# Telling TensorE's sequencer ahead of time which way each expert pair's branch goes

## The chip, the cores and the metric

The kernel runs on one core of one Trainium2 chip. The metric is the device time of one execution in microseconds (us), median of the runs shown. TensorE, VectorE, ScalarE, GpSimd and SyncE (the queue that issues most transfers) each have a sequencer of their own, which reads that engine's instruction stream, takes its branches, and hands the work to the engine.

## The reference, cut to what matters

One layer of a hybrid backbone over 256 latent tokens of 1024 channels. A first half (convolution branch, neighbourhood attention branch, recurrent branch, gates, output projection) is followed by a mixture of experts, which is where the change lies:

```python
gate = jnp.einsum("blk,blke->ble", w_sel, jax.nn.one_hot(e_idx, N_EXPERTS, dtype=f32)).astype(h.dtype)
out = jnp.zeros_like(h)
for e in range(N_EXPERTS):                       # 16 experts, hidden width 512
    he = jax.nn.silu(h @ w1[e]) * (h @ w3[e])
    out = out + gate[..., e:e + 1] * (he @ w2[e])
```

Each token goes to 2 of the 16 experts (the best two of its best group of four), so an expert gets few of the 256 tokens.

## The kernel before

**Two experts at a time.** The 16 experts are worked off as 8 pairs, p = 0 to 7. Each expert has 64 slots; `gather` fills them with its tokens' channels by products with one-hot matrices. For each pair TensorE makes the first product (`product(p, 0, ph0)`, the slots times w1), the second one (`product(p, 1, ph)`, times w3), turns the hidden rows (`hidden`), multiplies them by w2 (`rows`), and adds the result to the tokens (`scatter`, L1197). Of a product there are 8 steps, one for each 128 channels; in the trace a step is 4 weight loads and 4 matmuls, so a product is 32 of each, all on line L1162. The last pair is done by halves of the columns.

**The pairs overlap.** In the loop over p the first product of pair p + 1 is a generator, `w1`: two of its steps are issued behind `rows(p)`, then comes `scatter(p)`, then the six others, and then the next pass of the loop begins with the branch on pair p + 1.

**The branch.** An expert may get over 64 tokens. `cnt` holds the larger count of each pair. `values_load` puts it into a register of every engine (a TENSOR_LOAD, L1317 or L1322), and `tc.If(counts[p] > 64)` (L1323 for pairs 2 to 6, L1311 through `more` for pairs 0, 1 and 7) chooses. When it holds, `extra(p, 64)` works 32 more slots, and inside it `further(p, 96)`, `further(p, 128)` and so on stand nested, down to 224; each is a branch of its own. When it doesn't hold, every engine has to jump over the code of all six chunks. In `second` the second product stands in both arms of the If; for pairs 0, 1 and 7 the second product stands behind it. With this input one pair (5) has more than 64 tokens and none more than 96.

**The weights.** The experts' weights (192 quarters of a matrix, 512 KB each) go into 35 places, in the order of use. `load_experts` issues as many as `freed(n)` has granted; each issue waits on SyncE's queue until the place's last reader is done, and for an earlier transfer, as eight are under way at most.

Of the kernel before, what the change touches and what calls it, by code (L numbers as in the profile page):

```python
# [18 lines left out]
T = 256  # L19
# [7 lines left out]
# Columns of the packed per-channel vectors.  # L27
# [9 lines left out]
# Column blocks of the input projection, in units of 128.  # L37
CA, CGA, CQ, CK, CV, CRX, CRG, CG = 0, 4, 8, 12, 16, 20, 24, 28

# Places of 4 KB a partition, and of 1 KB and 2 KB for what is short-lived.  # L40
NPC, NRAW, NW, NSG, NSQ = 35, 4, 2, 6, 2
# How far the gates run ahead of their branches, and the scores of the values.
# [8 lines left out]
def tile_kernel(ctx, tc, x_all, cc, vecs, mod_a, mod_b, w_k, w_rx, w_v, w_in, rnn_w, rpb_t, w_br, w_out,  # L51
# [42 lines left out]
    def by4(dt=F32, name="b4"):  # L94
        """Eight blocks of T in two pieces: block k of them is f(k)."""
        ts = [cut(piece(dt, name), 0, [4, T]) for _ in range(2)]
        return lambda k: ts[k // 4][:, k % 4, :]

    # The experts' weights, a quarter of a matrix at a time: [pair][matrix][quarter][expert of the pair].
    ew = [[[[None, None] for _ in range(4)] for _ in range(3)] for _ in range(8)]  # L100
    # Those of the last pair are cut by their columns: half of the first two's come first, a quarter of the third's.
# [3 lines left out]
    # These come last before the experts' turn, into places that are free only then, and for a short while.  # L105
# [11 lines left out]
    def load_experts(n=192):  # L117
        """The next quarters, n at most, as long as there is room."""
        while n and room[0] > 0 and ew_order:
            p, i, q, s = ew_order.pop(0)  # L120
            n_ = loaded[0]
            loaded[0] += 1
            # the places of the other weights take their share
            make = piece if n_ % SPAN < OWN else w_tile if n_ % SPAN < OWN + XW else raw_tile
            load_expert(p, i, q, s, make(F32, "ew"), pool if n_ < OWN else nc.sync)
            room[0] -= 1
            n -= 1

    # The weights in the order in which they are used.
# [14 lines left out]
    # Each gate's projection runs LAG pairs of channel blocks ahead of its branch's product.  # L144
# [15 lines left out]
    # The last modulation weights have places of their own, from when the branches are done with theirs.  # L160
# [10 lines left out]
    # What has been loaded and not been used: weights, and modulation weights.  # L171
# [23 lines left out]
    def split_parts():  # L195
        """The split of the next weights, in two steps."""
# [26 lines left out]
    def load_ma_half(i, j):  # L223
        """Those of one k tile: 128 columns of the scale, and of the shift."""
# [45 lines left out]
    # before[i, j] = j < i, for ties that go to the first  # L270
# [12 lines left out]
    def rsqrt(srcs, n, scale):  # L283
        """1 / sqrt(ps * scale + eps) for n values a partition: a first guess from the bits, then Newton."""
# [13 lines left out]
        # y (15 - 10 x y^2 + 3 x^2 y^4) / 8, left at 8 / 3 of its size  # L298
# [9 lines left out]
    def spread(rs, n, name):  # L308
        """[token, n tiles] as rows of tokens, the same on every partition: [128, n * 128] in PSUM."""
# [20 lines left out]
    # adds the two halves of the rows below, and turns them  # L330
# [4 lines left out]
    class Mod:  # L335
        """Scale and shift of 256 channels, or of half j of them."""
# [6 lines left out]
        def products(self, ns=range(KD // 2)):  # L343
            # even and odd k tiles on different groups of the array's columns
# [54 lines left out]
    class Channels:  # L399
        """The normed tokens' channels of k tile k, in two parts."""  # L400
# [20 lines left out]
    def proj_block(ps, w, k, cols, both, start, stop):  # L421
        """Adds block `cols` of one k tile of the weights to ps: latents, then the context."""
# [6 lines left out]
    # Work of the other engines that fills the time of the projections, in two chains; what has been  # L429
    # asked of TensorE and of VectorE, in us, says when more of it is due.  # L430
# [48 lines left out]
    # The engines' turns, by the order in which the modulation's weights arrive.  # L479
# [46 lines left out]
    def mod_round_b(out, bank):  # L526
        """The modulation of 256 columns of each of the four quarters."""
# [18 lines left out]
    def set_g1(m, col):  # L546
        # half: the gated branches are summed at twice their size
        dve.tensor_scalar(g1[:, m:m + 1], col, v("mod_b", 16 + m), 0.5, op0=ALU.add, op1=ALU.mult)
# [29 lines left out]
    def gated_inputs():  # L578
        """The inputs of the convolution's and of the recurrence's output products."""
# [4 lines left out]
    def taps(b):  # L584
# [3 lines left out]
        for j in range(31):  # L588
            o = j - 15
            if o:  # L590
                # the tokens that have this neighbour
# [76 lines left out]
    def rnn(h):  # L668
        """Both directions of channel blocks 2 h and 2 h + 1."""
# [29 lines left out]
        # together, as they bring in a table of their own  # L699
# [57 lines left out]
    att_out = []  # L757

    def attention():
# [5 lines left out]
        # The heads' sums of squares, each block's on a group of the array's columns: [head, token], then turned.  # L765
# [131 lines left out]
    def shift_sums():  # L897
        """The part of the second norm's shift in the router's sums, the same for every token."""
# [49 lines left out]
    # The second norm's factor is left until the tokens are on partitions, its shift until the channels are.  # L948
# [22 lines left out]
    for m in range(KD):  # L971
# [16 lines left out]
        else:  # L988
            act.activation(sq2, xl[:, m, :], AF.Square)
            # brings in the table that the router's scores need  # L990
# [18 lines left out]
    # The last modulation vector is needed by the experts' rows only.  # L1009
# [21 lines left out]
    def ranks(x, n, name):  # L1031
        """How many of the four come before each one in x [128, n, 4], the first of equals first."""
# [14 lines left out]
    # A group's score is its largest sum of two.  # L1047
# [29 lines left out]
    # The scores and the masks go first.  # L1077
# [21 lines left out]
    def one_hot(e0):  # L1099
        """Slots 1 to 64 of four experts."""  # L1100
# [6 lines left out]
    def gather(oh, w, place):  # L1107
        """The tokens in their w slots: place(k) becomes [channel, w]."""
# [15 lines left out]
    def quarter(p, i, s, k, h):  # L1124
        """Rows k and half h of the columns of a matrix of an expert: its tile, and where in it."""
# [5 lines left out]
    # Room for the experts' rows, and for what leads to them.  # L1131
# [5 lines left out]
    def slots(p, oh, w):  # L1137
        """The slots' tokens, and the weights of the first 2 w slots: w of either expert."""
# [14 lines left out]
    def product(p, i, ph, h=None):  # L1153
        """The slots times one of the two matrices of the hidden rows, or half h of its columns."""
# [18 lines left out]
    def hidden(q):  # L1173
        """Half of the hidden rows, turned."""
# [5 lines left out]
    def rows(p, py, f, q):  # L1180
        """The experts' rows."""
# [8 lines left out]
    def scatter(rows_, toks, ms=range(KD), parts=2):  # L1190
        """The rows, added to the tokens that they belong to."""
# [12 lines left out]
    def extra(p, n, rest_=iter(())):  # L1204
        """Slots n + 1 to n + 32 of experts 2p and 2p + 1. The array's four column groups take an expert and half
        of the columns each. The steps of rest_ fill TensorE's time."""
# [8 lines left out]
        # the slots on partitions, then the channels  # L1215
# [58 lines left out]
        else:  # L1274
            # the places of the rows' parts still hold weights
# [18 lines left out]
    # Pieces that the experts' weights leave to the rest: the tokens, two groups' slots, the rows, the chunks  # L1294
    # beyond the first.
# [11 lines left out]

    def further(p, n):
        """The chunks from slot n + 1 on, as long as there are tokens for them."""
        if n < T:  # L1310
            with tc.If(counts[p] > n):  # L1311
# [3 lines left out]
    def more(p):  # L1315
        """The tokens of pair p beyond the first 64 of an expert."""
        counts[p] = nc.values_load(cnt[0:1, p:p + 1], min_val=0, max_val=T)  # L1317
        further(p, 64)

    def second(p, ph0, ph):  # L1320
        """The second product, and what there is of more(p)."""
        counts[p] = nc.values_load(cnt[0:1, p:p + 1], min_val=0, max_val=T)  # L1322
        with tc.If(counts[p] > 64) as c:  # L1323
# [22 lines left out]
    # The first products follow the tokens' channels.  # L1346
    ph0 = mm_bank(name="ph0")
    opening = open_group(0)
    next(opening)
    w1 = product(0, 0, ph0)  # L1350
# [8 lines left out]
    for p in range(7):  # L1359
# [4 lines left out]
        else:  # L1364
            # before the second product, as places are wanted
# [22 lines left out]
        # the rows' parts are waited for behind a little of the next product  # L1388
        ahead(w1, 2)
        scatter(lambda i, m: ys[i][:, m * 128:m * 128 + 128], lambda m: oT_)  # L1390
        run(w1)

# [34 lines left out]
def layout(x, c, ctx, c_ctx, router_w, router_bias, mod_w, mod_b, norm1_g, norm2_g, in_w, in_b, conv_dw_w,  # L1427
           conv_dw_b, conv_ln_g, conv_ln_b, conv_pw_w, na_q_g, na_k_g, na_rpb, na_out_w, rnn_conv_w,
           rnn_conv_b, rnn_wa, rnn_ba, rnn_wx, rnn_bx, rnn_lam, rnn_out_w, out_w, exp_w1, exp_w3, exp_w2):
    """The inputs as the program reads them; elements are only moved."""  # L1430
# [114 lines left out]
```

## Time and profile before

| | us |
|---|---|
| median of 3 runs | 641.96 |
| lowest and highest run | 639.98, 643.71 |
| span of the profiled execution, from first to last instruction | 640.2 |
| median less that span | 1.8 |
| TensorE busy in it | 586.9 (92%) |
| VectorE, ScalarE, GpSimd busy | 349.3, 260.0, 19.4 |

The trace tells the profiled execution's span; what a run's time has around the span is not in the trace, so the median less the span stands for it. A line of a timeline reads: start, duration, engine, line of the kernel, operation, out<-in by the program's names, partitions x elements, count, and in brackets the time for which the engine was idle before it and what ended that. An engine name with a q (PEq, PEldq, SPq, ACTq) is that engine's sequencer: it loads registers, waits, branches or issues, and the engine does nothing by it. PEld is TensorE loading weights, which overlaps with matmuls.

### The profile page before, as it was taken

What the parts mean: (1) busy time and instruction counts of PE and PEld (TensorE: products, weight loads), DVE (VectorE), ACT (ScalarE), POOL (GpSimd) and SP (SyncE); (2) the same over time, 40 slices, a digit from 0 to 9 for tenths busy, and PEclk for the clock granted to TensorE, in tenths of its full rate; (3) what the DMA queues carried; (4) which work ended last, traced back from release to release, by engine and by line L of the source; (5) the groups of instructions that cost most, each with busy time, mean ns of one, the idle gap of its engine ahead of it and who ended that gap; (6) DMA issues with size and microseconds to landing.
All of it is one profiled execution on the core that took longest, in us unless ns stands there. A gap on an engine that the chain in (4) does not pass through costs nothing. (4 is left out here: it accounts for less than half of the span.)

```text
span 640.2 us, 10603 instructions
## 1 busy us (share of the span) xinstructions
PE 586.9 (92%) x4127; PEld 411.5 (64%) x4127; DVE 349.3 (55%) x797; ACT 260.0 (41%) x456; POOL 19.4 (3%) x42
## 2 busy tenths in 40 slices
PE   1899999999999999999999989898989599998977
PEld 1689888768788869887999843353335245443454
DVE  4667999999688959885686541202221214222303
ACT  4335357373799647876455342021103011030101
POOL 0000000000000001022020100000000000000000
PEclk9999999999999999999999989999999899999979
DMA  8973974336742634679698759999999979489921
GB/s 255 376 305 141 312 249 153 130 138 232 262 162 102 225 138 149 224 283 349 226 346 303 234 216 368 346 334 407 354 407 409 407 252 412 170 298 408 408 109 67
DMA packets 51826, 170.68 MB, mean 267 GB/s; under 512 B 5664, under 2 KB 10016, under 8 KB 51744
## 3 DMA queue, kind: packets, MB, share of 16 engines
q1 hardware_dynamic: 46704, 151.26, 64.1%
q0 software_dynamic: 5040, 18.35, 8.1%
q8 instruction: 48, 0.79, 0.5%
q14 instruction: 34, 0.28, 0.1%
HBM read 168.54 MB, written 1.05 MB: 265 GB/s over the span
## 5 line engine op out<-in xcount | busy, mean ns | idle before, releaser
L1162 PE MATMUL ph<-ew,xg 128*64 128x512 f32 (+1 forms) x576 | 121.6, 570 | 21.3 <-issue 12.2
L1162 PEld LDWEIGHTS ph<-ew,xg 128*64 128x64 f32 x576 | 44.4, 143 | 86.8 <-issue 75.5
L73 ACT ACTIVATE w<-raw 128x1024 fp32r<-128x1024 f32 x68 | 71.8, 1057 | 65.0 <-PE gps L69 11.6
L74 DVE TENSOR_TENSOR w<-raw,w 128x1024 fp32r<-128x1024 f32 x68 | 82.9, 1219 | 21.1 <-ACT w L73 20.5
L1171 DVE SCALAR_TENSOR_TENSOR he<-sl,gsl,ph 128x256 f32<-128x256 f32 x16 | 7.1, 477 | 100.9 <-PE ph L1162 99.9
L70 PE MATMUL gps<-h,w 128*128 128x256 f32 x192 | 55.2, 288 | 1.1 <-DVE w L74 1.1
L68 PE MATMUL gps<-h,w 128*128 128x256 f32 x192 | 55.9, 291 | 0.4 <-DVE y L934 0.4
L69 PE MATMUL gps<-h,w 128*128 128x256 f32 x192 | 54.5, 284 | 0.0
L593 DVE SCALAR_TENSOR_TENSOR cacc<-up,vc,cacc 128x243 f32<-128x243 f32 (+14 forms) x120 | 52.1, 470 | 1.4 <-ACT cacc L585 0.7
L1183 PE MATMUL py<-ew,heT 128*64 128x512 f32 x224 | 49.6, 595 | 1.1 <-ACT heT L1178 0.8
L74 DVE TENSOR_TENSOR ys<-py,ys 128x512 fp32r<-128x512 f32 (+1 forms) x18 | 11.4, 632 | 58.0 <-ACT ys L73 58.0
L68 PEld LDWEIGHTS gps<-h,w 128*128 128x128 f32 x192 | 36.6, 191 | 4.1 <-issue 2.6
L70 PEld LDWEIGHTS gps<-h,w 128*128 128x128 f32 x192 | 36.7, 191 | 2.8 <-issue 1.5
L69 PEld LDWEIGHTS gps<-h,w 128*128 128x128 f32 x192 | 36.7, 191 | 0.9 <-issue 0.7
L1183 PEld LDWEIGHTS py<-ew,heT 128*64 128x64 f32 x224 | 15.5, 137 | 30.7 <-issue 25.9
L1201 DVE SCALAR_TENSOR_TENSOR xl<-scp,g,xl 128x256 f32<-128x256 f32 x72 | 29.2, 475 | 7.5 <-PE scp L1197 7.5
L1167 ACT ACTIVATE sl<-ph 128x512 f32<-128x512 f32 (+1 forms) x9 | 4.9, 550 | 67.3 <-PE ph L1162 52.8
L73 ACT ACTIVATE ys<-py 128x512 fp32r<-128x512 f32 (+1 forms) x18 | 9.9, 550 | 50.4 <-PE py L1183 36.5
L114 POOL DMA_DIRECT2D ew<-in_w_exp x31 | 16.6, 537 | 321.7 <-ACT pp L813 249.5
L1119 ACT ACTIVATE xg<-gps,b2m 128x256 f32<-128x256 f32 x32 | 13.4, 471 | 28.6 <-PE gps L1115 27.6
L349 PE MATMUL mps<-ma,cs 128*32 128x256 f32 (+1 forms) x160 | 10.1, 397 | 13.4 <-DMA ma<-in_mod_a 13.3
L1115 PEld LDWEIGHTS gps<-oh,hT 128*128 128x128 f32 x128 | 16.1, 194 | 6.5 <-issue 5.7
(358 smaller groups left out, 1310.4 us busy)
## 6 DMA issues: line engine op xcount, KB each, us to landing
ew<-in_w_exp SPq DMA_DIRECT2D x161, 512.0 KB, 10.2
raw<-in_w_in SPq DMA_DIRECT2D x40, 512.0 KB, 4.3
ew<-in_w_exp POOLq DMA_DIRECT2D x31, 512.0 KB, 7.7
raw<-in_mod_b SPq DMA_DIRECT2D x28, 512.0 KB, 4.1
ma<-in_mod_a SPq DMA_DIRECT2D x12, 512.0 KB, 10.5
raw<-in_w_br SPq DMA_DIRECT2D x12, 512.0 KB, 4.4
raw<-in_w_out SPq DMA_DIRECT2D x8, 512.0 KB, 7.6
ma<-in_mod_a SPq DMA_DIRECT2D x8, 256.0 KB, 6.9
```

Of the source, the lines that this page charges most:

```text
L68: pe.matmul(ps, wh, xh, start=start, stop=False, skip_group_check=True)
L69: pe.matmul(ps, wh, xl_, start=False, stop=False, skip_group_check=True)
L70: return pe.matmul(ps, wl, xh, start=False, stop=stop, skip_group_check=True)
L73: act.activation(hi, src, AF.Copy)
L74: dve.tensor_tensor(lo, src, r32(hi), op=ALU.subtract)
L114: queue.dma_start(t, w_exp[6 * p + 2 * i + s, :, 1024 * q:1024 * q + 1024])
L593: dve.scalar_tensor_tensor(cacc[:, b, i0:i1], up[:, b, i0 + o:i1 + o], half_d[:, b * 31 + j:b * 31 + j + 1], cacc[:, b, i0:i1], op0=ALU.mu ...
L1115: pe.matmul(ps[:, j, :], hT[i][t][:, k * 128:k * 128 + 128], oh[t], start=(j == 0 and t == 0 and i == 0), stop=(t == 1 and i == 1), skip_g ...
L1119: act.activation(place(k0 + j), ps[:, j, :], AF.Identity, bias=b2m[:, k0 + j:k0 + j + 1])
L1162: pe.matmul(ph[64 * s:64 * s + 64, cols], xg(k)[:, c:c + 64], w[:, at], start=k == 0 and not h, stop=k == KD - 1, skip_group_check=True)
L1183: pe.matmul(py[q][64 * s:64 * s + 64, :], heT[f // 2][:, f % 2, 64 * s:64 * s + 64], ew[p][2][f][s][:, q * 512:q * 512 + 512], start=f == ...
L1201: dve.scalar_tensor_tensor(xl[:, m, :], ps[:, j, :], g2[:, m:m + 1], xl[:, m, :], op0=ALU.mult, op1=ALU.add)
```

## The change

Every engine's register with the count of pair p + 1 is loaded behind `scatter(p)`, and no more at the branch. One step of the first product later, a mark is set for TensorE alone: the condition of the branch that comes is worked out from the register, and the sequencer is told by it which way the branch labelled `more{p+1}` will go. After the mark five steps of the first product follow, and then the branch. For pair 0 the register is loaded and the mark set behind the first step of the first `gather`. The branches carry the labels; the branches inside the extra chunks (from 96 on) have none.

```diff
+    def count(p):
+        counts[p] = nc.values_load(cnt[0:1, p:p + 1], min_val=0, max_val=T)
+
+    def expect(p):
+        tc.mark_branch_hint_location(f"more{p}", hint=counts[p] > 64, engines=(mybir.EngineType.PE,))
+
     def further(p, n):
         if n < T:
-            with tc.If(counts[p] > n):
+            with tc.If(counts[p] > n, label=f"more{p}" if n == 64 else None):
                 extra(p, n)
                 further(p, n + 32)
 
     def more(p):
-        counts[p] = nc.values_load(cnt[0:1, p:p + 1], min_val=0, max_val=T)
         further(p, 64)
 
     def second(p, ph0, ph):
-        counts[p] = nc.values_load(cnt[0:1, p:p + 1], min_val=0, max_val=T)
-        with tc.If(counts[p] > 64) as c:
+        with tc.If(counts[p] > 64, label=f"more{p}") as c:
             extra(p, 64, product(p, 1, ph))
...
     opening = open_group(0)
     next(opening)
+    count(0)
+    expect(0)
     w1 = product(0, 0, ph0)
...
         ahead(w1, 2)
         scatter(lambda i, m: ys[i][:, m * 128:m * 128 + 128], lambda m: oT_)
+        count(p + 1)
+        ahead(w1, 1)
+        expect(p + 1)
         run(w1)
```

## Rows read from the trace of the kernel before

**Rows 1.** The page: traffic in 40 slices of the span, 16.0 us each.

```profile
GB/s 255 376 305 141 312 249 153 130 138 232 262 162 102 225 138 149 224 283 349 226 346 303 234 216 368 346 334 407 354 407 409 407 252 412 170 298 408 408 109 67
```

**Rows 2.** TensorE's branches and register loads: duration ns min/median/max, first and last start.

```profile
L1311 PEldq COMPARE_BRANCH  x4: 3416/4885/6132, 377.6 to 605.3; - x4
...
L1323 PEldq COMPARE_BRANCH  x6: 82/6061/6167, 440.6 to 579.5; - x6
...
L1322 PEldq TENSOR_LOAD <-cnt x5: 300/304/313, 440.2 to 579.1; - x5
```

**Rows 3.** The same columns for single stretches: pairs 1 and 5.

```profile
L1311 ACTq COMPARE_BRANCH  x1: 45/45/45, 403.2 to 403.2; - x1
...
L1311 PEldq COMPARE_BRANCH  x1: 6128/6128/6128, 407.9 to 407.9; - x1
...
L1317 PEldq TENSOR_LOAD <-cnt x1: 313/313/313, 407.5 to 407.5; - x1
...
L1323 PEldq COMPARE_BRANCH  x1: 82/82/82, 532.9 to 532.9; - x1
...
L1311 PEldq COMPARE_BRANCH  x1: 3416/3416/3416, 557.8 to 557.8; - x1
```

**Rows 4.** Timeline of TensorE around the branches of pairs 0 to 7.

```profile
381.58 1.19 PE L1115 MATMUL gps<-oh,hT 128*128 128x256 f32 x8 [1.32 <-PEq L1311]
...
406.53 5.37 PE L1162 MATMUL ph<-ew,xg 128*64 128x512 f32 x24
414.24 8.78 PE L1162 MATMUL ph<-ew,xg 128*64 128x512 f32 x32 [2.34 <-PEq L1311]
...
446.92 7.09 PE L1162 MATMUL ph<-ew,xg 128*64 128x512 f32 x32 [2.31 <-DMA ew<-in_w_exp]
...
474.08 7.09 PE L1162 MATMUL ph<-ew,xg 128*64 128x512 f32 x32 [2.27 <-issue]
...
510.58 8.60 PE L1162 MATMUL ph<-ew,xg 128*64 128x512 f32 x32 [7.77 <-issue]
...
585.72 7.09 PE L1162 MATMUL ph<-ew,xg 128*64 128x512 f32 x32 [2.17 <-issue]
...
604.38 2.81 PE L1162 MATMUL ph<-ew,xg 128*64 128x256 f32 x24
611.58 9.32 PE L1162 MATMUL ph<-ew,xg 128*64 128x256 f32 x64 [4.39 <-PEq L1311]
...
621.20 3.67 PE L1162 MATMUL ph<-ew,xg 128*64 128x256 f32 x32
```

**Rows 5.** Timeline of TensorE's weight loads behind pair 4's branch.

```profile
505.00 0.13 PEld L1162 LDWEIGHTS ph<-ew,xg 128*64 128x64 f32 x1 [3.07 <-issue]
510.58 0.29 PEld L1162 LDWEIGHTS ph<-ew,xg 128*64 128x64 f32 x3 [5.45 <-issue]
```

**Rows 6.** DMA in 40 slices of a stretch: 553 to 562, then 498.5 to 511.

```profile
GB/s 0 0 0 0 0 0 0 0 0 0 0 0 0 0 0 0 0 0 0 0 0 0 0 0 0 73 0 0 0 0 0 36 0 0 0 0 0 0 0 73
...
DMA packets 1389, 5.08 MB, mean 407 GB/s; under 512 B 155, under 2 KB 155, under 8 KB 1386
```

**Rows 7.** Timeline of VectorE: last part of the rows, ahead of pairs 1 and 7.

```profile
403.50 0.69 DVE L74 TENSOR_TENSOR ys<-py,ys 128x512 fp32r<-128x512 f32 x1 [2.74 <-ACT ys L73]
...
602.17 0.69 DVE L74 TENSOR_TENSOR ys<-py,ys 128x512 fp32r<-128x512 f32 x1 [2.67 <-ACT ys L73]
```

**Rows 8.** Second products, pairs 1, 3: busy PE, PEld, DVE, ACT, POOL, PEclk, DMA share, GB/s.

```profile
414.20:423.10 8.90, 8.86 (x33) 3.29 (x34) 0.00 (x0) 0.00 (x0) 0.00 (x0) 0.81 0.76 219
...
474.00:481.20 7.20, 7.12 (x33) 2.75 (x33) 0.00 (x0) 0.00 (x0) 0.00 (x0) 1.00 1.03 407
```

**Rows 9.** Issues of pair 5's w1 quarters, their landing, and TensorE's timeline there.

```profile
L114 SPq DMA_DIRECT2D ew<-in_w_exp x8: 327/328/328, 492.5 to 501.5; - x8
...
DMA to landing us min/median/max: 11.1/11.1/11.1
...
527.70 1.89 PE L1162 MATMUL ph<-ew,xg 128*64 128x512 f32 x8
```

## The prediction

> **What bounds the kernel now.** I read the page first. Over the span TensorE is busy 586.9 of 640.2 us, and in the experts' part (from 370 on) it is the engine everything waits for. So I asked what its idle time there ends with. In the timeline of TensorE the reader is to look at the brackets: in front of the second product of pairs 1, 2, 3, 4, 6 and 7 the array stands idle for 2.34, 2.31, 2.27, 7.77, 2.17 and 4.39 us, and 1.32 us in the middle of pair 0's opening [rows 4]. The releasers named there differ (a sequencer, a transfer, "issue"), so I looked for what they share. The sequencer's own instructions tell it: a register load of 0.3 us and then a compare-and-branch, which takes about 6.1 us on TensorE [rows 2]. The same branch takes 45 ns on ScalarE, and 82 ns on TensorE where the extra chunk is wanted (pair 5) [rows 3]. So it is no compare that costs: it is the jump over the skipped code. In a stretch in which the weights' transfers rest, the only traffic is instruction packets, one of them about 1 us after the branch at 557.8, and that branch takes 3.4 us; in the stretch of pair 4's branch transfers run at 407 GB/s [rows 3, 6]. I read this as a fetch of the code at the jump's target, slowed by the weights.
>
> Why only 2.3 of 6.1 us is seen: pair 1's branch starts at 407.9, and the array works off the first product until 406.53 + 5.37 = 411.90 [rows 3, 4]. At the register load (407.5) about 4 of those 24 weight load and matmul couples are done, so the sequencer is 20 couples ahead, worth 20/24 of 5.37 = 4.5 us. That queue is the cover.
>
> Pair 4 is a case of its own. Its branch, 6.08 us from 498.8, is over at 504.9; one weight load runs at 505.00 and then nothing until 510.58, though no data are missing [rows 2, 5]. I take that as a second fetch: the target lies just ahead of the end of a piece of code, and the next piece isn't there. So 7.77 = 2.2 (first fetch) + 5.58 (second).
>
> **The change part by part.**
>
> *The register load moves* from the branch to behind the scatter: 0.31 us, with what follows about 0.4 from its start to the branch's [rows 3]. It then runs while the queue is full, so the branch starts 0.4 earlier: 0.4 in each of 7 gaps, 2.9 in all, contained in the gaps below. On ScalarE and VectorE it stands between the same neighbours as before; SyncE and GpSimd issue no transfer between the old place and the new.
>
> *Mark and register arithmetic are added*, on TensorE's sequencer alone, 8 times. The trace has neither. Below: a branch that isn't taken, 0.08; above: a taken one, 6.1, if the sequencer stands still for the fetch. Nothing suggests that a mark gains by itself. As it tests a register and asks for something, it is nearest to the register load; I take 0.3. The 4.5 us of queued couples hide it; without that cover it would be 2.4 in all.
>
> *The fetch begins at the mark.* How much earlier is that? The mark stands 20 couples ahead of the branch. If the sequencer is held back by the full queue it goes at the array's pace: 4.5 us, at half width (pair 7) 20/24 of 2.81 = 2.3. If it was waiting for the second half of the rows and then catches up, it goes faster: they are done at 403.50 + 0.69 = 404.19, and from then to the register load at 407.5 it issues 8 couples of the scatter and 24 of the product, so 20 couples take 20/32 of 3.3 = 2.0 us; for pair 7 from 602.86 to 604.9, 1.3 us [rows 2, 3, 7]. The remainder at the branch is then 6.1 - 4.5 = 1.6 to 6.1 - 2.0 = 4.1, against a cover of 411.9 - 407.5 = 4.4. So pairs 1, 2, 3 and 6 lose the whole gap, at the lower bound just so: behind the branch the array needs 0.2 more (414.0 to 414.24). I leave 0.2 in each of these and in pair 4, 1.0. Pair 0's mark stands over 30 couples ahead and its branch is a short one (the median 4.885 of four is the mean of it and of pair 1's 6.128, so 3.64 [rows 2, 3]): 1.32 goes.
>
> *Pair 7*: remainder 6.13 - 2.3 = 3.8 to 6.13 - 1.3 = 4.8; cover 604.38 + 2.81 - 604.9 = 2.3. A gap of 1.5 to 2.5 stays of 4.39; I take 2.3 off.
>
> *Pair 4*: five marks with their arithmetic stand ahead of its target, so the code behind moves on by some places, and the target passes into the next piece. Both fetches go: 7.77. Whether another target moves to a piece's end the trace doesn't show; that is a rival.
>
> *The clock.* [...] Without idle array time ahead of them 1.69 + 1.51 + up to 1.98 come back; as pair 7 keeps a gap I take 1.5 of the last. Sum 4.7.
>
> *Sum*: 1.32 + 2.34 + 2.31 + 2.27 + 2.17 = 10.4; pair 4 7.8; pair 7 2.3; clock 4.7; less 1.0: 24.2 us. From the profiled 640.2 that is 616.0, with 1.8 around the span 617.8: **618 us**, 3.7% under the median of 641.96.
>
> [...]
>
> **What the gain runs into.** TensorE comes up to 19 us earlier to pair 5. Its first w1 quarters are issued at 492.5, the last at 501.5, and land 11.1 later, 503.6 to 512.6; they were wanted from 527.70 and would be from about 508.5, the last ones from about 516 [rows 9]. That leaves 3 to 5 us, and more if the transfers start earlier, as they do after pair 1. Between 480 and 512 they run at 409 and 407 GB/s [rows 1], so they can't be hurried: up to pair 5 a gain over some 22 us would be lost again. The sum has 19.
>
> **The rivals.**
>
> *The mark fetches nothing.* Then the gaps shrink by the moved load alone, 2.9, and pair 4's target still moves (5.6, and with a gap of 1.8 its 1.5 of clock): 10.0, so 632. For it: nothing in this trace shows a fetch ahead of a jump; each of these branches starts its wait anew. Against it: code on the straight way does come ahead of use, since TensorE is nowhere else in the experts' part without work or data.
> [...]
>
> *Another entry falls at a piece's end*, or the weights come late at pair 5. A second fetch costs 5.6 and 1.5 of clock, 7.1: 625. One of seven entries had it before.
>
> *Both at once*, no fetch and a new bad entry: 10.0 - 7.1 = 2.9, 639, which is no change.
>
> *The mark holds the sequencer* until its fetch is done, and the branch fetches again. Then each mark costs 6.1 less the 4.5 queued, 1.6 for five pairs, 3.8 at half width, perhaps 1 for pair 0: 12.8 more, and about three falls of the clock at 1.7, against 10.0 gained: 648. It decides once the mark takes over 5 us. Against it: an engine that is told ahead has no reason to wait.
>
> **How the numbers follow.** Forecast 0.66 (own range 612 to 624: all of pair 7 given back at the one end, another 1 us left in each of six gaps at the other); another entry or late weights 0.10; no fetch 0.15; both 0.05; the mark holds 0.04. Under 0.5% (3.2 us) a measurement of this kernel can't tell from no change. The range of 612 to 634 takes in the first three. Faster 0.89, leaving a little of the third case out; same 0.06; slower 0.05.
>
> **What the profile after would show.** TensorE's branches of pairs 0 to 4, 6 and 7 at 0.1 to 4 us in place of 3.6 to 6.1, pair 7's the longest remainder; pair 5's inner branch, which has no label, still at 3.4. No idle bracket over 0.5 us in front of the second products but pair 7's. No stall between the first and second weight load of pair 4. The granted clock at its upper level in the second products of pairs 1 and 4. If the branches still take 6.1 the mark does nothing; if they are short and the array waits for transfers, the weights have become the bound; if a gap of some 5 us opens behind a short branch, it is an entry at a piece's end.

## The result and the profile after

| | before | after |
|---|---|---|
| median, us | 641.28 (4 runs, 639.98 to 643.71) | 618.73 (4 runs, 616.12 to 620.48) |
| ratio with 95% interval | | 0.9626 [0.9589, 0.9663] |
| span of the profiled execution | 640.2 | 614.3 (its time 616.12) |
| TensorE busy | 586.9 (92%) | 580.2 (94%) |

The change takes 22.6 us off the median; the quotient of the two medians, 0.965, is within the interval given. The two profiled executions differ by more, 25.9 us, mostly because the one of after is the fastest of its four.

TensorE's sequencer after, as in [rows 2]: duration in ns (min/median/max), first and last start. L1318 and L1328 are the branches, L1313 the register arithmetic, L1541 the marks.

```profile
L1318 PEldq COMPARE_BRANCH  x4: 3341/3572/4750, 375.9 to 583.0; - x4
...
L1328 PEldq COMPARE_BRANCH  x6: 89/3688/4074, 435.4 to 559.6; - x6
...
L1541 PEldq BRANCH_PREFETCH_HINT  x8: 37/40/44, 372.7 to 581.6; - x8
...
L1313 PEldq ALU_OP  x8: 37/37/48, 372.6 to 581.5; - x8
```

Where the branches of the middle pairs took 6.1 us they take 3.5 to 4.1. Single stretches tell why: mark and branch of pair 1, of pair 7, pair 5's inner branch, and pair 0's branch.

```profile
L1541 PEldq BRANCH_PREFETCH_HINT  x1: 40/40/40, 403.0 to 403.0; - x1
...
L1318 PEldq COMPARE_BRANCH  x1: 3694/3694/3694, 405.5 to 405.5; - x1
...
L1541 PEldq BRANCH_PREFETCH_HINT  x1: 40/40/40, 581.6 to 581.6; - x1
...
L1318 PEldq COMPARE_BRANCH  x1: 4750/4750/4750, 583.0 to 583.0; - x1
...
L1318 PEldq COMPARE_BRANCH  x1: 3341/3341/3341, 538.5 to 538.5; - x1
...
L1318 PEldq COMPARE_BRANCH  x1: 3451/3451/3451, 375.9 to 375.9; - x1
```

From pair 1's mark to the end of its branch pass 405.5 + 3.69 - 403.0 = 6.2 us, from pair 7's 583.0 + 4.75 - 581.6 = 6.15: the same 6.1 that the branch alone took before. The wait has not become shorter, it starts at the mark, 2.5 us ahead of the branch in pair 1 and 1.4 in pair 7. The code packets (16 KB each, the DMA view's queue q8) say the same: pair 1's begins 3.6 us behind the start of the branch before (at 411.47), and 3.7 us behind the mark after (at 406.71). Pair 0's branch, 3.45 us, is nearly what it was (3.64).

What the array makes of it, in TensorE's timeline, as [rows 4]:

```profile
379.63 1.18 PE L1115 MATMUL gps<-oh,hT 128*128 128x256 f32 x8 [0.54 <-PEq L1318]
...
404.58 5.37 PE L1162 MATMUL ph<-ew,xg 128*64 128x512 f32 x24
410.11 2.80 PE L1162 MATMUL ph<-ew,xg 128*64 128x512 f32 x12 [0.16 <-PEq L1318]
413.67 4.51 PE L1162 MATMUL ph<-ew,xg 128*64 128x512 f32 x20 [0.76 <-issue]
...
434.45 12.24 PE L1162 MATMUL ph<-ew,xg 128*64 128x512 f32 x56
...
459.14 12.24 PE L1162 MATMUL ph<-ew,xg 128*64 128x512 f32 x56
...
487.60 12.24 PE L1162 MATMUL ph<-ew,xg 128*64 128x512 f32 x56
...
558.66 12.26 PE L1162 MATMUL ph<-ew,xg 128*64 128x512 f32 x56
...
582.49 2.81 PE L1162 MATMUL ph<-ew,xg 128*64 128x256 f32 x24
587.91 7.13 PE L1162 MATMUL ph<-ew,xg 128*64 128x256 f32 x64 [2.61 <-PEq L1318]
```

In pairs 2, 3, 4 and 6 the end of the first product and the whole second one stand in one line of 56 = 24 + 32 couples: no gap is left to print. Pair 4's 5.6 us stall behind its first weight load [rows 5] is gone with it. Pair 7 keeps 2.61, and pair 1 has a new stall of 0.76 after 12 couples of its second product.

The windows of the second products of pairs 1 and 7 (columns as in [rows 8]) show a mean granted clock of 1.00:

```profile
410.10:418.30 8.20, 7.43 (x33) 3.00 (x34) 0.01 (x1) 0.60 (x1) 0.00 (x0) 1.00 0.99 363
587.90:595.10 7.20, 7.19 (x65) 5.50 (x66) 0.48 (x1) 0.41 (x2) 0.00 (x0) 1.00 0.73 287
```

The weights still come in time, though they are asked for earlier. The page's traffic by slices of 15.4 us, to be held against [rows 1]:

```profile
GB/s 256 367 339 114 310 259 154 137 141 193 278 212 103 138 241 103 236 176 356 313 211 379 283 245 226 388 360 406 402 393 407 407 408 409 398 226 409 409 248 68
```

and, among the waits, all that the product's weight loads wait for a transfer in the experts' part (us in total, times, longest):

```profile
PEld ph L1162 <- DMA ew<-in_w_exp: 2.5, 9, 0.3
```

### The profile page after: what moved, and what is told of

It reads as the page before. It is cut to its first block, busy times and chain, and to the rows that moved or that the text cites. A ratio compares the mean times of both kernels' runs of the same rounds, so it can differ in the third digit from the quotient of the medians.

```text
span 614.3 us, 10619 instructions
## 1 busy us (share of the span) xinstructions
PE 580.2 (94%) x4127; PEld 408.1 (66%) x4127; DVE 349.1 (57%) x797; ACT 259.8 (42%) x456; POOL 19.4 (3%) x42
## 5 line engine op out<-in xcount | busy, mean ns | idle before, releaser
L1162 PE MATMUL ph<-ew,xg 128*64 128x512 f32 (+1 forms) x576 | 115.6, 548 | 3.5 <-PEq L1318 2.8
L1162 PEld LDWEIGHTS ph<-ew,xg 128*64 128x64 f32 x576 | 41.5, 137 | 66.0 <-issue 58.3
L1197 PEld LDWEIGHTS scp<-oT,ys 128*128 128x128 f32 x128 | 15.7, 188 | 6.7 <-issue 5.2
```

The source lines that it names most:

```text
L1162: pe.matmul(ph[64 * s:64 * s + 64, cols], xg(k)[:, c:c + 64], w[:, at], start=k == 0 and not h, stop=k == KD - 1, skip_group_check=True)
L1197: pe.matmul(ps[:, j, :], rows_(i, m), toks(m), start=(j == 0 and i == 0), stop=i == parts - 1, skip_group_check=True)
```

## The experiments

All were compared with the kernel before on the same chip (its medians there: 641.71, 642.07 and 641.45 in the three groups), so ratios can be compared across groups.

### Only the load is moved

```diff
     count(0)
-    expect(0)
...
         ahead(w1, 1)
-        expect(p + 1)
```

> The counts are loaded early as in the changed kernel, but no mark is set; the code behind stands where it stood before. Theory (the mark does the work): TensorE's taken branches stay at 6.1 us for pairs 1 to 4, 6 and 7, each starts 0.4 us earlier, gaps shrink by 0.4 each, pair 4 keeps its second stall of 5.6: about 2.9 us gained, some 638 us. Rival (the early load alone does it): the gaps go, below 625.

Measured: 638.91, ratio 0.9968 [0.9945, 0.9991]. Its branches and the timeline of its pair 4:

```profile
L1328 PEldq COMPARE_BRANCH  x6: 82/6116/6221, 436.5 to 574.7; - x6
```

```profile
506.25 8.63 PE L1162 MATMUL ph<-ew,xg 128*64 128x512 f32 x32 [7.78 <-issue]
```

The branches take what they took. The gaps of pairs 1, 2, 3, 6 and 7 shrink by 0.3 to 0.5 each and pair 0's by 0.85, while pair 4's stays. The earlier load is worth 2.8 us by the medians and 2.1 by the ratio, whose interval reaches from 0.6 to 3.5.

### The mark always says that the branch falls through

The same instructions at the same places; only the answer is changed.

```diff
-        tc.mark_branch_hint_location(f"more{p}", hint=counts[p] > 64, engines=(mybir.EngineType.PE,))
+        tc.mark_branch_hint_location(f"more{p}", hint=counts[p] > 0, engines=(mybir.EngineType.PE,))
```

> All marks are set, from a register too, but they always say that there will be no jump (the condition is a count over 0). Instructions and their places are those of the changed kernel. Theory (the mark starts the fetch of the target): branches at 6.1 us as before, gaps of 1.8 to 1.9 for pairs 1, 2, 3, 6 and 4.0 for pair 7, but pair 4's second stall of 5.6 is gone, since the target has moved by ten places: about 632 us (629 to 635). Rival one (any mark helps): about 619. Rival two (pair 4's second stall is not of the code's places): pair 4 keeps a gap over 7 and the time is about 638.

Measured: 631.15, ratio 0.9845 [0.9804, 0.9885].

```profile
L1328 PEldq COMPARE_BRANCH  x6: 80/6055/6242, 436.8 to 567.9; - x6
```

```profile
500.26 7.09 PE L1162 MATMUL ph<-ew,xg 128*64 128x512 f32 x32 [1.81 <-issue]
```

The branches are at 6.06 again, so what shortens them in the change is what the mark says, not that something stands there. And pair 4's gap is 1.81, its product 7.09, where the moved load alone left 7.78 and 8.63: the second stall and the slow product go with the added instructions, which move the target, whatever they say. So the 22.6 us come in three parts: 2.8 from the load (641.7 to 638.9), 7.8 from the moved target (638.9 to 631.15; pair 4 alone shows 7.78 - 1.81 + 8.63 - 7.09 = 7.5), and 12.4 from the fetch begun at the mark (631.15 to 618.73). They add up to 23.0, as the last median comes from another group of runs.

### The mark says the opposite

`counts[p] < 65`: wrong for all eight pairs, with a needless jump announced for pair 5.

> The changed kernel with the condition of the mark turned round: no jump is told for the seven pairs that jump, a jump for pair 5, which doesn't. Theory (a wrong mark for a jump that isn't taken puts a needless fetch in front of the next piece of code): as with marks that always say no jump, 631 us, and in pair 5 one stall of up to 6 us: 631 to 637. Rival (a wrong mark costs nothing there): 631 us and no new gap in pair 5.

Measured: 630.54, ratio 0.9819 [0.9773, 0.9866]; the branches:

```profile
L1328 PEldq COMPARE_BRANCH  x6: 89/5986/6197, 438.5 to 568.5; - x6
```

The same as marks that never announce a jump, within the intervals. The jump announced for pair 5, which doesn't come, made no new gap (in front of the next gather the array waits 0.56 us, 0.85 in the change); its inner branch even takes 0.34 us in place of 3.34. Why was not shown. The 0.6 us between the medians are inside the spread.

### The mark 48 couples ahead, and 80

`count(p + 1)` and `expect(p + 1)` are put ahead of `ahead(w1, 2)` and the scatter (48 couples before the branch), or ahead of the rows (80).

```diff
         freed(8)
+        count(p + 1)
+        expect(p + 1)
         ahead(w1, 2)
         scatter(lambda i, m: ys[i][:, m * 128:m * 128 + 128], lambda m: oT_)
-        count(p + 1)
-        ahead(w1, 1)
-        expect(p + 1)
```

> Load and mark ahead of the first two steps of the first product, 48 couples ahead of the branch in place of 20 (pair 0 as in the changed kernel). Theory (the fetch runs from the mark on its own and takes about 6 us from it): the target is there when the branch comes, TensorE's branches of pairs 1 to 4 and 6 under 0.5 us, pair 7's under 1, pair 7's gap of 2.6 and pair 1's 0.8 go: 615 us. Rival (the fetch is only brought forward in the queue and the branch still waits 3.5 us, or the mark lapses when a new piece of code begins): branches of 3.5 to 6 us, 619 to 622.

> Load and mark ahead of the rows of the pair before, 80 couples ahead of the branch. Theory: as with 48, branches under 0.5 us, 615 us. Rival (a mark lapses when the sequencer goes on to another piece of code, which 80 couples do in more than every second pair): some branches are back at 6.1 and their gaps at 2 us, 619 to 626.

Measured: 614.19, ratio 0.9578 [0.9551, 0.9606], at 48; 615.23, ratio 0.9590 [0.9562, 0.9618], at 80. The branches at 48, all and then pair 2's and pair 3's alone:

```profile
L1328 PEldq COMPARE_BRANCH  x6: 89/646/3317, 434.2 to 558.5; - x6
...
L1318 PEldq COMPARE_BRANCH  x4: 438/1882/3456, 375.7 to 581.9; - x4
...
L1328 PEldq COMPARE_BRANCH  x1: 3317/3317/3317, 434.2 to 434.2; - x1
...
L1328 PEldq COMPARE_BRANCH  x1: 653/653/653, 458.9 to 458.9; - x1
```

and the timeline of pairs 1 and 7:

```profile
409.99 7.09 PE L1162 MATMUL ph<-ew,xg 128*64 128x512 f32 x32 [0.16 <-PEq L1318]
...
584.38 7.30 PE L1162 MATMUL ph<-ew,xg 128*64 128x256 f32 x64 [0.16 <-PEq L1318]
```

Pair 7's gap is down from 2.61 to 0.16, pair 1's second stall is gone, and the branches of pairs 1, 3, 4 and 7 take 0.4 to 0.7 us, pair 6's 1.25. In pairs 2 and 3 the lead at 48 couples is 8.5 and 8.6 us, more than the 6.1 that a branch took; 80 couples are no better (615.23 against 614.19). That pair 2's branch keeps 3.32 us was not expected; at 80 couples it still takes 3.13. Pair 0's, whose mark stands where it did in the change, keeps 3.46 and 3.70. In the DMA view of pair 2 the line of the 16 KB code packets (q8: count, MB, share) has no packet between its mark at 425.7 and its branch at 434.2, and this one in the 3.3 us behind the branch's start; in pair 3 two come between mark and branch.

```profile
q8 instruction: 1, 0.02, 2.0%
...
q8 instruction: 2, 0.03, 1.6%
```

Pair 0's packet begins 1.0 us behind its branch's start, 0.9 in the kernel before, though the mark is set 3.1 us ahead of the branch. So in pairs 0 and 2 the early mark lay unused for a while, by these packets. It costs nothing in pair 2, whose 56 couples run in one line of 12.24 us.

### Moving the code by some places

The packets of q8, 16 KB each, are read as TensorE's code. In the straight part of the kernel before, from 27.3 to 362.4 us, the trace has one for each 252 of TensorE's recorded instructions (5048 over 20 packets). The places here are the author's estimate: a count in the built program, with a piece taken a little over these 252, as some records are missing. By it the branches of pairs 0 and 2 stand 16 and 35 places behind the start of their piece; no trace shows a place, and the count may be off by a few. Twelve further marks, with their arithmetic, are 24 instructions and move what stands behind them by as many places. First at pair 1, which was also to put pair 1's target 2 places ahead of a piece's end, where pair 4's was before; then at pair 0. Both start from the kernel with 48 couples.

```diff
-        expect(p + 1)
+        for _ in range(13 if p == 0 else 1):
+            expect(p + 1)
```

```diff
-    expect(0)
+    for _ in range(13):
+        expect(0)
```

> As the mark 48 couples ahead, but pair 1's mark is set 13 times over. In the built program each adds two of TensorE's instructions, so that pair 1's jump target, 26 places ahead of the end of a code piece in the kernel with the mark at 48, comes to stand 2 ahead of it; all later code moves on by 24 places. Theory (a target at a piece's end costs a second fetch): the branch of pair 1 stays short, but its second product stalls behind its first weight load for 3 us or more (a fetch of some 6 us less what is queued), about 617 us. Rival (that stall in the kernel before had another cause): no stall in pair 1, 614 us.

> The mark at 48 with all code from pair 1 on moved by the same 24 places as in the kernel with pair 1's thirteen marks, but the twelve extra marks stand in pair 0's opening, so each other pair has one. Theory one (what that kernel showed came of the places alone): pair 2's branch, which now stands 59 places into its piece and not 35, is under 1 us, pair 5 stalls by 2 us behind its eighth matmul after the jump back, pair 1 has no stall; 617 to 619 us. Theory two (pair 1's second fetch was brought by its thirteen marks): pair 1 now stalls by 2 to 3 us behind its first weight load, 619 to 622 us.

Measured: 617.91, ratio 0.9617 [0.9582, 0.9651], for the first; 621.91, ratio 0.9678 [0.9630, 0.9725], for the second. The first's timeline in pairs 1 and 5:

```profile
412.38 7.09 PE L1162 MATMUL ph<-ew,xg 128*64 128x512 f32 x32 [0.16 <-PEq L1318]
...
544.16 1.18 PE L1115 MATMUL gps<-oh,hT 128*128 128x256 f32 x8 [1.28 <-ACT sl L1167]
...
547.34 4.49 PE L1115 MATMUL gps<-oh,hT 128*128 128x256 f32 x24 [1.99 <-issue]
```

The stall that was to come in pair 1 didn't, so the time is near the 617 of the theory for another reason. The code packets suggest why there was none. From behind the packet under way at pair 1's mark to pair 2's mark there are three with the mark at 48 (398.5 to 425.7), and two in the first kernel here (401.5 to 428.1):

```profile
q8 instruction: 3, 0.05, 0.7%
...
q8 instruction: 2, 0.03, 0.4%
```

In pair 4 the same step, from three packets before to two after (498.8 to 520, 488 to 512), goes with the end of its stall. Some 318 places lie between pair 1's target and pair 2's branch by the count; with 2 of them at a piece's end they would need three pieces. So by the packets and this estimate the 24 places carried pair 1's target past the end of its piece, and the run doesn't test an entry 2 places ahead of it. One stall came in pair 5 instead, after 8 products behind the jump back from the inner branch, whose target had moved to 19 places ahead of a piece's end by the count. In the second kernel pair 1 again has none, and pair 5 has it after 8 again (1.45 us). The second kernel's branches of pairs 0 and 2, and then its thirteen marks and what the array did meanwhile:

```profile
L1318 PEldq COMPARE_BRANCH  x1: 483/483/483, 381.5 to 381.5; - x1
...
L1328 PEldq COMPARE_BRANCH  x1: 433/433/433, 440.0 to 440.0; - x1
...
L1540 PEldq BRANCH_PREFETCH_HINT  x13: 30/30/44, 373.5 to 375.8; - x13
```

```profile
375.89 2.07 PE L1115 MATMUL gps<-oh,hT 128*128 128x256 f32 x8 [2.60 <-issue]
```

Pair 0's branch, moved by 24 places (to 40 by the count), falls from 3.46 to 0.48 us, pair 2's, moved by as many (to 59), from 3.32 to 0.43 (0.44 in the first kernel, where it is moved alike, with the same 48 couples of lead). The time falls into the range of theory two, whose stall is absent; it is above that of theory one because 12 further marks with their arithmetic, at 0.19 us each, run where nothing is queued: the array waits 2.60 us and then takes 2.07 and 3.68 us for the next two groups of 8 products, which take 1.20 and 1.94 in the kernel with 48 couples and one mark there.

### Half of the weights' traffic

The kernel before, but of each quarter of pairs 1 to 7 only half the columns are loaded and read twice; so half of these experts' weights are left out of the computation.

```diff
+        if p:
+            queue.dma_start(t[:, :512], w_exp[6 * p + 2 * i + s, :, 1024 * q:1024 * q + 512])
+            t = Half(t)
```

> The kernel before, without marks, but of the weights of pairs 1 to 7 only half of each quarter is loaded, and the products read that half twice: half the traffic, the same instructions on TensorE. Theory (the code's fetch stands behind the weights' packets): branches that fall in a rest of the transfers take 3.4 to 3.7 us in place of 6.1, and the gaps of pairs 1, 2, 3 and 6 go, pair 7's falls to some 1.7, pair 4's to 2 to 3: 619 to 624 us. Rival (a jump of this length takes 6.1 by itself): branches at 6.1 as before, about 640 us.

Measured: 623.52, ratio 0.9712 [0.9674, 0.9749].

```profile
L1335 PEldq COMPARE_BRANCH  x6: 82/3304/4381, 436.9 to 566.8; - x6
...
L1323 PEldq COMPARE_BRANCH  x4: 3268/3718/3829, 377.4 to 590.5; - x4
```

Without any mark the branches fall from 6.1 to between 3.3 and 4.4 us, with a median of 3.3, about what pair 5's inner branch takes while the transfers rest (3.42 before). So some 2.8 of the 6.1 us are read as the code packet standing behind the weights' packets: pair 1's packet begins 1.0 us behind the branch's start here, where it was 3.6. Gaps of 0.16 and 0.53 us stay in pairs 1 and 2, 2.52 in pair 4 and 1.53 in pair 7.

### A mark for the inner branch too

The kernel with 48 couples; the branch on chunk 96 gets a label, and inside `extra(p, 64)` a mark some 200 couples ahead of it. Beside it ran the changed kernel once more.

```diff
+        if n == 64:
+            tc.mark_branch_hint_location(f"again{p}", hint=counts[p] > 96, engines=(mybir.EngineType.PE,))
```

> The mark 48 couples ahead, and besides a mark at the start of each extra chunk from 64 on for the branch on the next chunk, which one pair runs. Theory: that branch (3.3 us, a gap of 0.83 behind it) becomes short, 0.8 us less than with the mark at 48 alone, 613.4 us. Rival (a mark some 200 couples ahead lapses, since the code goes on to another piece before the branch): the branch stays at 3.3 and the time at 614.2.

> The changed kernel itself, beside the others on the same chip: 618.7 us, so that the kernels with earlier marks stand 4 us under it. Rival (the earlier mark's gain is the scatter of the runs): within 1.5 us of the kernel with the inner mark.

Measured: 614.08, ratio 0.9580 [0.9545, 0.9614]; the changed kernel 619.57, ratio 0.9667 [0.9626, 0.9709]. The inner branch and what the array waited for behind it:

```profile
L1320 PEldq COMPARE_BRANCH  x1: 351/351/351, 537.9 to 537.9; - x1
```

```profile
542.20 4.03 PE L1115 MATMUL gps<-oh,hT 128*128 128x256 f32 x32 [1.27 <-DVEq L1320]
```

The branch falls from 3.34 to 0.35 us, and nothing is gained: the profile puts the end of the gap down to VectorE's sequencer, as it did with the mark at 48 alone, and the gap is 1.27 where it was 0.83. What VectorE's side waits for was not followed up; its branches take 0.05 to 0.07 us in the change. At 0.35 us, a mark some 200 couples ahead still shortens its branch. The changed kernel repeats its time, and the two intervals don't overlap: the 28 couples of further lead are worth 4.5 to 5.5 us by the medians (618.73 to 614.19, 619.57 to 614.08) and 3 to 5.6 by the ratios. This time the changed kernel's pair 7 worked its second product in 8.81 us against the 7.13 shown above, behind the same gap (2.65): the 1.7 us between them are gained in one execution and not in the other.

## Why the prediction was right

The time came out 0.7 us above the forecast, by the likeliest case, and the steps can be held against the rows one by one.

| step | predicted off, us | in the profiled executions |
|---|---|---|
| gaps of pairs 1, 2, 3, 6 | 9.1 - 0.8 | 8.2 (pair 1 keeps 0.16 + 0.76, the others nothing) |
| pair 0 | 1.3 | 0.8 (0.54 stays) |
| pair 4, both fetches | 7.8 - 0.2 | 7.8 |
| pair 7 | 2.3 | 1.8 (2.61 stays) |
| clock, pairs 1, 4, 7 | 1.7 + 1.5 + 1.5 | 1.5 + 1.5 + 2.2 |
| sum | 24.2 | 23.7 |

Of the 25.9 us between the two spans 1.2 more lie ahead of pair 0's branch, where nothing was changed (the products behind it start 1.95 earlier, 0.78 of it the gap); the last 1.0 is spread and not assigned. The column is that of the change's fastest execution. In its second profiled one (617.9 us, 22.3 less than before) the same rows sum to 21.9: pair 0 gives 0.4 and pair 7's clock 0.5. That the sum came within 1 us is in part luck in these two terms.

**The fetch begins at the mark.** Right, and shown by the answer alone being changed, 12.4 us, and by the code packet that follows the mark by 3.7 us. The rival that the mark fetches nothing is what the kernel with a false answer does, at 631.15 where 632 was worked out. Its branches take 6.06 us (median), those marked with the right answer 3.7 and, 48 couples ahead, 0.4 to 0.7 in four of the pairs.

**How far ahead.** Of the two readings the faster sequencer is the right one. The lead was 2.5 us in pair 1, where the prediction's ends were 2.0 and 4.5, and 1.4 in pair 7 (1.3 and 2.3); the remainders of 3.5 to 4.1 and 4.75 stand at the upper ends given. Pair 7's term was taken from between the ends and came out 0.5 too large.

**The cover.** Behind a remainder of 3.5 to 4.1 us the queued couples hide all in pairs 2, 3, 4 and 6; the 0.2 left in each wasn't needed. The mark and its arithmetic take 0.04 us each and 0.19 from one to the next, less than the 0.3 taken, and are hidden, but for the thirteen in pair 0's opening.

**Pair 4.** Right in size, and the gap goes as the code moves: 7.78 us with the load alone moved, 1.81 with marks that never announce a jump. That it was a second fetch at a piece's end is the author's reading; the code packets, three before and two after, speak for it. It is a third of the gain, and has nothing to do with telling the sequencer anything.

**The clock.** That the array's idle time lowers the clock and so costs these 4.7 us was the author's estimate; no run shows it by itself. What the runs show: before, the second products of pairs 1, 4 and 7 take 8.78, 8.60 and 9.32 us at mean granted clocks of 0.81 [rows 8], 0.82 and 0.76; after, pair 1's takes 2.80 + 4.51 us, pair 7's 7.13 behind 2.61 us of idle time, and pair 4's ends the line of 12.24 for 56 couples, all three at 1.00. In the changed kernel's other execution pair 7's took 8.81 behind 2.65. Pairs 4 and 7 before (columns as in [rows 8]):

```profile
510.50:519.20 8.70, 8.62 (x33) 3.51 (x33) 0.00 (x0) 0.00 (x0) 0.00 (x0) 0.82 0.64 226
611.50:621.00 9.50, 9.42 (x66) 6.21 (x66) 0.48 (x1) 0.06 (x1) 0.00 (x0) 0.76 0.11 44
```

**Pair 0** was mis-sized. Its whole gap was to go as its mark stands over 30 couples ahead; the branch only fell from 3.64 to 3.45. The gap shrank by the moved load: that alone brought it to 0.47, against 0.54 in the change. The place of the branch in its piece seems to decide: moved by 24 places it takes 0.48.

**Another entry at a piece's end.** In part: pair 1's second product stalls after 12 couples, its target being some 26 places ahead of a piece's end by the count, for 0.76 us rather than 5.6; the 12 couples that still run are 2.80 us of cover. The weights at pair 5 came in time.

**The mark holds the sequencer.** Wrong: 0.04 us. Branches not taken show 80 to 89 ns here, marked ones that jump 348 at the least. The mark at 48 couples measures 614.19 though its branches take 0.4 us and more: no gap over 0.16 us is left in front of the second products. The price of this rival is added up wrong in the prediction: 12.8 and three times 1.7 against 10.0 are 7.9 more than 641.96, which is 650 and not 648; nothing else hangs on it.

## What to carry to other kernels

The long compare-and-branch on one engine (6.1 us on TensorE, 0.04 to 0.07 on the others) is read here as a fetch of code at the jump's target; to tell the sequencer ahead moved the start of that wait, to the mark 2.5 us ahead in pair 1, so choose the lead from the measured wait (here 6.1 us), not from a count of products, and check how far ahead of the array the sequencer really runs. Added instructions also move every target behind them, by which a stall of 5.6 us went here and one of 2.0 came: measure the change with the answer falsified before crediting the mark. Here the mark 48 couples ahead (614.19, ratio 0.9578) is the version to keep.

## What was not expected of the hardware

- A mark seems to be acted on only when the sequencer has come to the piece of code in which the branch stands; this is a guess, with places by the author's count. For it: pair 2's branch, 35 places into its piece, keeps 3.1 to 3.6 us with the mark at 20, 48 and 80 couples, and takes 0.43 to 0.44 at 59 places; pair 0's, at 16, keeps 3.4 to 3.8 with its mark 3.1 us ahead, and takes 0.48 at 40; the code packets of both begin only behind the branch's start, pair 0's by 1.0 us. In pair 2, 3.3 us left of 6.1 would be a start 2.8 us ahead of the branch. This is argued from five kernels; no run tried it by itself.
- Behind a jump 12 couples ran before a second stall in pair 1 (the change), 8 in pair 5 (both kernels with moved code) and one weight load in pair 4 (before). By the author's count, an estimate, these targets have 26, 19 and 2 places left in their piece, and a couple takes two. Pair 1's target, 24 places further on, brought no stall in two kernels: by the two code packets in place of three, seen in one of them, it stood in the next piece.
- A jump of this kind takes 3.4 to 3.6 us where transfers all but rest (5 GB/s around pair 5's inner branch, 20 around pair 0's) and 6.1 where they run at 378 GB/s (pair 1) and 407 (pair 4): nearly double.
- One needless jump announced cost nothing measurable (630.54 against 631.15 with marks that never announce one).
